# A two-layer hybrid decoder in float32: narrow matmuls for halved K, sums by a ones matmul, work moved to ScalarE, modulation paced by stage

## The chip, the cores and the metric

The kernel runs on one core of one Trainium2 chip. The metric is the device time of one launch in microseconds (us), the median of several runs. PE is TensorE, DVE is VectorE, ACT is ScalarE, POOL is GpSimd, SP is SyncE, whose queue issues the weight transfers.

## What is computed

Two decoder layers on 256 tokens of width 2048, in float32. Layer 0 mixes tokens by gated linear attention (GLA), layer 1 by softmax attention with a forget bias (FoX). After each mixer comes a gated MLP with a causal convolution of width 3. Every sub-layer's input is normalised, scaled and shifted, and its output gated, by vectors that are a product of the condition `c` with `w_mod` (2 x 2048 x 12288, some 200 MB).

```python
def reference(x, c, ...):
    cond = jax.nn.silu(c)
    for i in range(DEPTH):
        mod = (cond @ w_mod[i] + b_mod[i])[:, None, :]
        sh_m, sc_m, g_m, sh_f, sc_f, g_f = jnp.split(mod, 6, axis=-1)
        h = rmsnorm(x, norm_mix[i]) * (1.0 + sc_m) + sh_m
        ...                                   # y = gla_mixer(h, ...) or fox_mixer(h, ...)
        x = x + (1.0 + g_m) * y
        h = rmsnorm(x, norm_ffn[i]) * (1.0 + sc_f) + sh_f
        x = x + (1.0 + g_f) * conv_ffn(h, ffn_w_up[i], ffn_conv_w[i], ffn_conv_b[i], ffn_w_down[i])
    return rmsnorm(x, norm_final)
```

## The kernel before

Activations lie transposed: 16 tiles of 128 features by 256 tokens. Each float32 operand of the large products is split in two, a high part (the value rounded to fp32r) and a low part (the rest), and a product is high x high + high x low + low x high.

*Weights.* `next_w` takes the next weight tile (0.5 MB) of a list written out ahead (`plan`): SP loads it into one of five ring buffers, ACT casts it to the high part (line 110), DVE subtracts for the low part (line 111), up to three tiles ahead of use. `stream_p` (line 544) multiplies: a tile holds two K rows of 512 columns, so 8 blocks of 128 x 128. In a block the high part of the weights meets high and low operand side by side, 512 columns (line 554), and the low part the high operand, 256 columns (line 555). The two halves of the result stand next to each other in a double bank of PSUM, two such banks for a group of 512 columns, of three that there are; `gather` adds them up. `stream_b` (line 587) does the same for products whose result has tokens in rows. `narrow` (line 605) is a 16-column product by three 256-column matmuls (lines 614 to 616).

*Stages.* For GLA and the first six column groups of layer 0's up-projection, K is cut in two halves of 8 tiles (`BLOCKS`, `FIRST`), all columns for the first half and then all for the second, whose partial results are added in SBUF by DVE (line 582). So the first half can start before scale and shift of the second are known. In order: the start (0 to 62 us), GLA's products, first half to about 209 and second half to 390, GLA out (to 500), layer 0's up-projection (514 to 1025, the halved groups until 796), its down-projection (to 1283), FoX's products and attention (to 1718), FoX out (to 1814), layer 1's up-projection (to 2325) and down-projection.

*Modulation.* `mod_tasks` makes tasks of one `w_mod` tile (0.5 MB, in the same ring), each a product of the tile with a column of the condition, added up on DVE in `acc` (line 250 the first, line 252 the others). After 16 tiles a column sum over the partitions is wanted: `finish` transposes `acc` (line 265) and sums each block with an accumulating activation on ACT (line 274), or at the start with a reduction on DVE. The tasks wait in a queue; `tick`, called after each weight tile, takes as many as `pace["bg"]` says (0.64 means 64 for 100 weight tiles), and small pieces of other work (convolutions, attention heads) at the pace `pace["side"]`. `set_pace(n)` spreads what is queued over n weight tiles. `between` empties the queue between the two halves of the up-projection.

*Operands.* `make_h` makes the normalised, scaled and shifted operand h, 16 pieces per stage, on demand: DVE product (line 464), ACT for the high part (line 465), DVE again for the unrounded value (line 466), DVE for the low part (line 467). `token_rstd` is the reciprocal root before it (lines 426 to 434). `raw_operand` (lines 482, 483) splits the others.

*Order.* Each engine works off its own queue in order. The order in each queue is set when the program is built, by a planner that simulates the program with its own costs, within the data's dependences and the limits that the kernel adds by hand (`issue_after`).

## Time and profile before

| | us |
|---|---|
| median of 3 runs | 2592.15 (2590.53 to 2594.13) |
| the profiled execution | 2593.84 |
| its span, first to last instruction | 2592.1 |

The profile is one execution, recorded by the hardware. A row of a table by stage gives the stretch, its length, then for each engine its busy time and the number of instructions, then the granted TensorE clock as a share of 2.4 GHz, the mean busy share of the 16 DMA engines, and GB/s. A row of a timeline gives start, duration, engine, line, operation, the tiles that it writes and reads, and in brackets how long the engine stood idle before and what ended the wait. A matmul's duration includes its way through the array: the distance between two starts says what one costs in a row of them. A row of instruction groups gives busy time, mean ns of one, and idle time before them.

### The profile page before, as it was taken

To read this page: it belongs to the slowest core of one execution; us is meant where nothing else is said; L and a number is where in the kernel's file an instruction comes from. 1 tells how busy PE (TensorE), PEld (TensorE's weight loads), DVE (VectorE), ACT (ScalarE), POOL (GpSimd) and SP (SyncE) were. 2 spreads that over 40 slices of the span, in tenths; PEclk is the share of its full clock that TensorE was granted. 3 is DMA by queue.
4 is the path that set the end of the run, shared out by engine and by line. 5 is a ranking of instruction groups with operands and counts; after the bars stand their busy time and mean duration, and the time that the engine had idled before them with its cause. 6 is when DMAs were issued, how large, how long until landed. Compare 5 with 4: busy or idle time off the path is not lost.

```text
span 2592.1 us, 36814 instructions
## 1 busy us (share of the span) xinstructions
PE 2486.6 (96%) x13738; PEld 2139.2 (83%) x13738; DVE 2010.2 (78%) x2784; ACT 1288.2 (50%) x1964; POOL 18.1 (1%) x35
## 2 busy tenths in 40 slices
PE   6999998899999999899999999999899999999998
PEld 6887887788888888788888888778788888888887
DVE  7877988888789999877587888877877777767554
ACT  2447353445555565443454555543655555565332
POOL 0000000000000000000000000100000000000000
PEclk7999998899999999999999999999999999999999
DMA  8896877789567888898589988768577777765653
GB/s 335 276 311 218 294 235 255 247 293 324 178 186 259 295 295 295 269 305 299 178 267 307 305 269 229 215 228 267 171 221 229 226 224 225 223 196 195 191 189 116
DMA packets 267727, 637.67 MB, mean 246 GB/s; under 512 B 23449, under 2 KB 24459, under 8 KB 267164
## 3 DMA queue, kind: packets, MB, share of 16 engines
q1 hardware_dynamic: 267160, 635.17, 75.3%
q8 instruction: 108, 1.77, 0.3%
q14 instruction: 71, 0.58, 0.1%
q10 hardware_dynamic: 388, 0.15, 0.0%
HBM read 633.14 MB, written 2.10 MB: 245 GB/s over the span
## 4 chain that ended last, share of the span: by engine, by line
PE 72%; DVE 12%; DMA 10%; issue 3%; ACT 3%; DVEq 0%; SPq 0%; ACTq 0%
PE pa L554 38%; PE pa L555 19%; DMA wm<-in_w_mod_dram 7%; DVE wl L111 4%; PE pa L601 4%; PE pa L599 4%; PE pa L600 4%; DVE acc L252 3%; ACT wh L110 1%; DVE xT L624 1%; DMA w<-in_ffn_w_down_dram 1%; DMA w<-in_gla_w_in_dram 1%; DMA w<-in_ffn_w_up_dram 0%; PE pm L411 0%; PE pm L265 0%
## 5 line engine op out<-in xcount | busy, mean ns | idle before, releaser
L110 ACT CAST wh<-w 128x1024 fp32r<-128x1024 f32 x819 | 856.2, 1049 | 986.5 <-PE pa L554 429.5
L111 DVE TENSOR_TENSOR wl<-w,wh 128x1024 fp32r<-128x1024 f32 x819 | 994.4, 1218 | 368.0 <-ACT wh L110 361.4
L554 PE MATMUL pa<-h,wh 128*128 128x512 f32 x3584 | 1264.4, 399 | 15.9 <-DVE h L467 7.8
L555 PE MATMUL pa<-h,wl 128*128 128x256 f32 x3584 | 992.8, 282 | 6.7 <-DVE wl L111 6.6
L554 PEld LDWEIGHTS pa<-h,wh 128*128 128x128 f32 x3584 | 671.4, 189 | 169.3 <-ACT h L465 8.1
L555 PEld LDWEIGHTS pa<-h,wl 128*128 128x128 f32 x3584 | 681.9, 190 | 21.9 <-DVE wl L111 9.4
L554 PE MATMUL pa<-op,wh 128*128 128x512 f32 x1920 | 676.0, 398 | 18.9 <-DVE op L483 14.8
L555 PE MATMUL pa<-op,wl 128*128 128x256 f32 x1920 | 531.9, 281 | 4.2 <-DVE wl L111 4.2
L252 DVE SCALAR_TENSOR_TENSOR acc<-wm,cT,acc 128x1024 f32<-128x1024 f32 x352 | 450.7, 1280 | 104.9 <-DMA wm<-in_w_mod_dram 103.9
L554 PEld LDWEIGHTS pa<-op,wh 128*128 128x128 f32 x1920 | 359.8, 189 | 103.6 <-DVE op L483 15.2
L555 PEld LDWEIGHTS pa<-op,wl 128*128 128x128 f32 x1920 | 363.9, 190 | 9.5 <-DVE wl L111 6.0
L600 PE MATMUL pa<-wh,h 128*128 128x512 f32 x512 | 201.6, 394 | 0.0
L599 PE MATMUL pa<-wh,h 128*128 128x512 f32 x512 | 200.7, 393 | 0.0
L601 PE MATMUL pa<-wl,h 128*128 128x512 f32 x512 | 197.5, 394 | 0.1
L1081 ACT ACTIVATE y<-u,cw 128x256 f32<-128x256 f32 x176 | 99.0, 597 | 37.3 <-DVE u L585 22.0
L601 PEld LDWEIGHTS pa<-wl,h 128*128 128x128 f32 x512 | 96.5, 189 | 20.1 <-DVE wl L111 0.4
L599 PEld LDWEIGHTS pa<-wh,h 128*128 128x128 f32 x512 | 96.6, 189 | 19.3
L600 PEld LDWEIGHTS pa<-wh,h 128*128 128x128 f32 x512 | 96.5, 189 | 19.2
L1082 DVE SCALAR_TENSOR_TENSOR y<-u,cw,y 128x255 f32<-128x255 f32 x176 | 84.0, 477 | 0.0
L1084 DVE SCALAR_TENSOR_TENSOR y<-u,cw,y 128x254 f32<-128x254 f32 x176 | 82.6, 476 | 0.7
L585 DVE TENSOR_TENSOR u<-u,pa 128x512 f32<-128x512 f32 x112 | 75.7, 679 | 4.0 <-ACT u L584 3.9
L624 DVE SCALAR_TENSOR_TENSOR xT<-pa,mod,xT 128x256 f32<-128x256 f32 x128 | 53.1, 476 | 20.1 <-PE pa L555 20.1
(238 smaller groups left out, 1249.4 us busy)
## 6 DMA issues: line engine op xcount, KB each, us to landing
wm<-in_w_mod_dram SPq DMA_DIRECT2D x352, 512.0 KB, 5.1
w<-in_ffn_w_up_dram SPq DMA_DIRECT2D x352, 512.0 KB, 4.7
w<-in_ffn_w_down_dram SPq DMA_DIRECT2D x176, 512.0 KB, 5.1
w<-in_fox_w_in_dram SPq DMA_DIRECT2D x128, 512.0 KB, 5.3
w<-in_gla_w_in_dram SPq DMA_DIRECT2D x96, 512.0 KB, 4.9
wm<-in_w_mod_dram SPq DMA_DIRECT2D x16, 1024.0 KB, 12.3
w<-in_gla_w_out_dram SPq DMA_DIRECT2D x32, 512.0 KB, 5.5
w<-in_fox_w_out_dram SPq DMA_DIRECT2D x32, 512.0 KB, 5.6
```

Source lines behind the costliest of these rows:

```text
L110: nc.scalar.copy(out=hi, in_=src)
L111: order["v"] = nc.vector.tensor_tensor(out=lo, in0=src, in1=hi.bitcast(F32), op=ALU.subtract).ins
L252: nc.vector.scalar_tensor_tensor(out=st["a"], in0=wt[:, j, :], scalar=col, in1=st["a"], op0=ALU.mult, op1=ALU.add)
L554: nc.tensor.matmul(o, ws[0][:, ms], hl, start=first, stop=False, skip_group_check=True)
L555: nc.tensor.matmul(o[:, 0, :], ws[1][:, ms], hl[:, 0, :], start=False, stop=last, skip_group_check=True)
L599: nc.tensor.matmul(o, lh[:, ts_], wh[:, hs_], start=first, stop=False)
L600: nc.tensor.matmul(o, ll[:, ts_], wh[:, hs_], start=False, stop=False)
L601: nc.tensor.matmul(o, lh[:, ts_], wl[:, hs_], start=False, stop=last)
L624: nc.vector.scalar_tensor_tensor(out=xT[:, m, :], in0=ps[:, j, s_, :], scalar=modcol(l, key, m), in1=xT[:, m, :], op0=ALU.mult, op1=ALU.add)
L1081: nc.scalar.activation(y, u, AF.Identity, scale=cw[:, l * 3 + 2, r:r + 1], bias=cw[:, 6 + l, r:r + 1])
L1082: nc.vector.scalar_tensor_tensor(out=y[:, 1:], in0=u[:, :T - 1], scalar=cw[:, l * 3 + 1, r:r + 1], in1=y[:, 1:], op0=ALU.mult, op1=ALU.add)
L1084: nc.vector.scalar_tensor_tensor(out=y[:, 2:], in0=u[:, :T - 2], scalar=cw[:, l * 3, r:r + 1], in1=y[:, 2:], op0=ALU.mult, op1=ALU.add)
```

## The change

Seven edits. (1) `finish` multiplies each block of `acc` by a column of ones, one output column per block, and DVE adds the bias; where four K tiles were multiplied on PE already (`direct`), the sums go on top of them. (2) The first product of each `acc` is made on ACT. (3) In `token_rstd` the two token columns are computed together, three steps an iteration. (4) In `make_h`, for all pieces but the first two, ACT makes the scaled value and then its rounded copy; DVE keeps the first product and the low part. (5) `stream_p` gets a second form, `wide=False`, for the halved stages: three 256-column matmuls into one result, one double bank per group, which is copied or added as one instruction of 1024 columns. (6) In FoX, scalings of the normalised heads, the bias addition and the division by the row sum are made on ACT. (7) In layer 0's FFN the modulation pace is 0.3 per weight tile in the last part of the up-projection (0.64 before), and the rest is spread over the first 80 weight tiles of the down-projection; the side pace there is 1.0 (0.7 before).

```diff
-N1, N2, N3, N4 = 26, 151, 152, 156
+UPRATE = 0.3
+N1, N2, N3, N4 = 26, 80, 152, 156
...
                     elif k == direct:
                         st["a"] = accp.tile([P, 1024], F32, tag="acc", name=nm("acc"))[:, :width]
-                        nc.vector.tensor_scalar(out=st["a"], in0=wt[:, j, :], scalar1=col, scalar2=None, op0=ALU.mult)
+                        nc.scalar.activation(st["a"], wt[:, j, :], AF.Copy, scale=col)
...
-                red = tmp.tile([P, 8], F32, tag="red", name=nm("red"))
-                for q0 in range(0, mn, 4):
-                    pt = bank2("pt")[:, 0, :] if wide or defer else misc()
-                    for m in range(min(4, mn - q0)):
-                        nc.tensor.transpose(pt[:, m * P:(m + 1) * P], st["a"][:, (q0 + m) * P:(q0 + m + 1) * P],
-                                            ident)
-                    if wide:
-                        mq = min(4, mn - q0)
-                        nc.vector.tensor_reduce(out=red[:, q0:q0 + mq], in_=pt[:, :mq * P]
-                                                .rearrange("p (m k) -> p m k", k=P), axis=AX.X, op=ALU.add)
-                        continue
-                    for m in range(min(4, mn - q0)):
-                        blk = pt[:, m * P:(m + 1) * P]
-                        nc.scalar.activation(blk, blk, AF.Copy, accum_out=red[:, q0 + m:q0 + m + 1])
+                pt = st["p"] if direct else bank2("pt")[:, 0, :] if wide or defer else misc()
+                for m in range(mn):
+                    nc.tensor.matmul(pt[:, m:m + 1], st["a"][:, m * P:(m + 1) * P], one,
+                                     start=(m == 0 and not direct), stop=True, skip_group_check=True)
                 dst = mod[:, l * 6 + s, m0:m0 + mn]
                 b0 = l * 96 + s * KT + m0
-                nc.vector.tensor_tensor(out=dst, in0=red[:, :mn], in1=bm[:, b0:b0 + mn], op=ALU.add)
-                if direct:
-                    nc.vector.tensor_tensor(out=dst, in0=dst, in1=st["p"][:, :mn], op=ALU.add)
+                nc.vector.tensor_tensor(out=dst, in0=pt[:, :mn], in1=bm[:, b0:b0 + mn], op=ALU.add)
...
         for _ in range(3):
-            for i in range(2):
-                c1 = slice(i, i + 1)
-                nc.vector.tensor_scalar(out=t[:, c1], in0=q[:, c1], scalar1=q[:, c1], scalar2=v[:, c1],
-                                        op0=ALU.mult, op1=ALU.mult)
-            for i in range(2):
-                c1 = slice(i, i + 1)
-                nc.vector.tensor_scalar(out=q[:, c1], in0=t[:, c1], scalar1=1.5, scalar2=q[:, c1],
-                                        op0=ALU.subtract, op1=ALU.mult)
+            nc.vector.tensor_tensor(out=t, in0=q, in1=q, op=ALU.mult)
+            nc.vector.tensor_tensor(out=t, in0=t, in1=v, op=ALU.mult)
+            nc.vector.scalar_tensor_tensor(out=q, in0=t, scalar=1.5, in1=q, op0=ALU.subtract, op1=ALU.mult)
...
-            nc.scalar.activation(hi, t, AF.Identity, scale=sc, bias=sh)
-            nc.vector.tensor_scalar(out=t, in0=t, scalar1=sc, scalar2=sh, op0=ALU.mult, op1=ALU.add)
+            if m < 2:
+                nc.scalar.activation(hi, t, AF.Identity, scale=sc, bias=sh)
+                nc.vector.tensor_scalar(out=t, in0=t, scalar1=sc, scalar2=sh, op0=ALU.mult, op1=ALU.add)
+            else:
+                nc.scalar.activation(t, t, AF.Identity, scale=sc, bias=sh)
+                nc.scalar.copy(out=hi, in_=t)
             ins = nc.vector.tensor_tensor(out=lo, in0=t, in1=hi.bitcast(F32), op=ALU.subtract).ins
...
-    def stream_p(kts, c0, rhs, done=None):
-        ps = [bank2().rearrange("p j (s t) -> p j s t", s=2) for _ in range(2)]
+    def stream_p(kts, c0, rhs, done=None, wide=True):
+        ps = [bank2().rearrange("p j (s t) -> p j s t", s=2) for _ in range(2 if wide else 1)]
...
-            o = ps[m // 2][:, m % 2, :, :]
-            nc.tensor.matmul(o, ws[0][:, ms], hl, start=first, stop=False, skip_group_check=True)
-            nc.tensor.matmul(o[:, 0, :], ws[1][:, ms], hl[:, 0, :], start=False, stop=last, skip_group_check=True)
+            if wide:
+                o = ps[m // 2][:, m % 2, :, :]
+                nc.tensor.matmul(o, ws[0][:, ms], hl, start=first, stop=False, skip_group_check=True)
+                nc.tensor.matmul(o[:, 0, :], ws[1][:, ms], hl[:, 0, :], start=False, stop=last, skip_group_check=True)
+                return
+            o = ps[0][:, m // 2, m % 2, :]
+            nc.tensor.matmul(o, ws[0][:, ms], hl[:, 0, :], start=(first and m % 2 == 0), stop=False,
+                             skip_group_check=True)
+            nc.tensor.matmul(o, ws[0][:, ms], hl[:, 1, :], start=False, stop=False, skip_group_check=True)
+            nc.tensor.matmul(o, ws[1][:, ms], hl[:, 0, :], start=False, stop=last, skip_group_check=True)
...
-        return ps
-    def gather(dst, ps, add=False):
-        if add:
-            nc.vector.tensor_tensor(out=dst, in0=dst, in1=ps[:, :, 1, :], op=ALU.add)
-        else:
-            nc.scalar.copy(out=dst, in_=ps[:, :, 1, :])
+        return ps if wide else ps[0]
+    def gather(dst, ps):
+        nc.scalar.copy(out=dst, in_=ps[:, :, 1, :])
         nc.vector.tensor_tensor(out=dst, in0=dst, in1=ps[:, :, 0, :], op=ALU.add)
...
-            for b in range(4):
-                dst = parts[key][:, b, :]
-                if new:
-                    nc.scalar.copy(out=dst, in_=ps[b // 2][:, b % 2, :])
-                else:
-                    nc.vector.tensor_tensor(out=dst, in0=dst, in1=ps[b // 2][:, b % 2, :], op=ALU.add)
+            for tt in range(TT):
+                take(parts[key][:, 2 * tt:2 * tt + 2, :], ps[tt], new)
...
             for g in range(2):
-                ps = stream_p(kts, c0 + g * 512, h)
-                for b in range(2):
-                    gather(parts[key][:, g * 2 + b, :].rearrange("p (j t) -> p j t", j=2), ps[b], not new)
+                ps = stream_p(kts, c0 + g * 512, h, wide=False).rearrange("p j s t -> p j (s t)")
+                take(parts[key][:, 2 * g:2 * g + 2, :], ps, new)
+        def take(dst, ps, new):
+            if new:
+                nc.scalar.copy(out=dst, in_=ps)
+            else:
+                nc.vector.tensor_tensor(out=dst, in0=dst, in1=ps, op=ALU.add)
...
                             blk = (tt * 2 + hh // 4) * 4 + hh % 4
-                            nc.vector.tensor_scalar(out=tok4[:, blk, :], in0=tok4[:, blk, :],
-                                                    scalar1=rs[:, blk:blk + 1], scalar2=None, op0=ALU.mult)
+                            nc.scalar.activation(tok4[:, blk, :], tok4[:, blk, :], AF.Copy, scale=rs[:, blk:blk + 1])
...
-                nc.vector.tensor_scalar(out=s[:, 0:P], in0=p_[:, 0:P], scalar1=cumt[:, 0, hd:hd + 1],
-                                        scalar2=None, op0=ALU.add)
-                nc.vector.tensor_scalar(out=s[:, P:3 * P], in0=p_[:, P:3 * P], scalar1=cumt[:, 1, hd:hd + 1],
-                                        scalar2=None, op0=ALU.add)
+                nc.scalar.activation(s[:, 0:P], p_[:, 0:P], AF.Identity, bias=cumt[:, 0, hd:hd + 1])
+                nc.scalar.activation(s[:, P:3 * P], p_[:, P:3 * P], AF.Identity, bias=cumt[:, 1, hd:hd + 1])
...
-                nc.vector.tensor_scalar(out=s[:, 0:P], in0=s[:, 0:P], scalar1=mx[:, 6:7], scalar2=None, op0=ALU.mult)
-                nc.vector.tensor_scalar(out=s[:, P:3 * P], in0=s[:, P:3 * P], scalar1=mx[:, 7:8], scalar2=None,
-                                        op0=ALU.mult)
+                nc.scalar.activation(s[:, 0:P], s[:, 0:P], AF.Copy, scale=mx[:, 6:7])
+                nc.scalar.activation(s[:, P:3 * P], s[:, P:3 * P], AF.Copy, scale=mx[:, 7:8])
...
         def up(g, half, kts, add=False):
+            c0 = half * DFF + g * 512
             if half == 0 and not add:
                 us[g] = bigt([P, 8, T], "u")
-            ps = stream_p(kts, half * DFF + g * 512, h)
+            dst = us[g][:, half * 4:half * 4 + 4, :]
+            if kts is not ALL:
+                ps = stream_p(kts, c0, h, wide=False).rearrange("p j s t -> p (j s) t")
+                if add:
+                    nc.vector.tensor_tensor(out=dst, in0=dst, in1=ps, op=ALU.add)
+                else:
+                    nc.scalar.copy(out=dst, in_=ps)
+                return
+            ps = stream_p(kts, c0, h)
             for b in range(2):
-                m = half * 4 + 2 * b
-                gather(us[g][:, m:m + 2, :], ps[b], add)
+                gather(dst[:, 2 * b:2 * b + 2, :], ps[b])
...
+        down()
         add_residual(l, "g_f", list(range(FT)), rhs)
...
@@ -1240,7 +1240,14 @@
         queue(mod_tasks(0, "g_f"))
         queue_halves(1, "m")
         pace["bg"] = SLOW
-    ffn(0, lazy(make_h(0, "f"), KT, 2, (8,)), (ALL[:8], between, lambda: set_pace(N2)))
+    def after():
+        pace["bg"] = UPRATE
+    def down():
+        pace["side"] = 1.0
+        set_pace(N2)
+    ffn(0, lazy(make_h(0, "f"), KT, 2, (8,)), (ALL[:8], between, after), down)
```

## Rows read from the trace of the kernel before

**Rows 1.** The page, part 1: busy us, share of the span, instructions.

```profile
PE 2486.6 (96%) x13738; PEld 2139.2 (83%) x13738; DVE 2010.2 (78%) x2784; ACT 1288.2 (50%) x1964; POOL 18.1 (1%) x35
```

**Rows 2.** Table by stage, five stretches (columns as told above).

```profile
540.00:560.00 20.00, 20.00 (x116) 17.38 (x115) 17.91 (x17) 8.79 (x11) 0.00 (x0) 1.00 0.96 338
660.00:665.00 5.00, 4.89 (x15) 4.24 (x16) 5.00 (x16) 2.19 (x4) 0.00 (x0) 0.50 0.22 79
796.00:1025.00 229.00, 228.14 (x1308) 198.70 (x1307) 217.03 (x296) 134.41 (x212) 0.00 (x0) 1.00 0.87 294
1025.00:1283.00 258.00, 249.01 (x1422) 216.72 (x1422) 190.89 (x203) 111.45 (x152) 0.00 (x0) 0.99 0.83 277
1589.00:1718.00 129.00, 122.00 (x677) 101.95 (x676) 98.36 (x190) 67.32 (x133) 8.27 (x8) 0.97 0.74 203
```

**Rows 3.** Timeline of PE, seven entries before which it stood idle.

```profile
212.92 0.58 PE L614 MATMUL pm<-h,wh 128*128 128x256 f32 x1 [4.07 <-ACT h L465]
...
269.55 0.58 PE L555 MATMUL pa<-h,wl 128*128 128x256 f32 x1 [2.98 <-DVE wl L111]
...
413.10 0.79 PE L554 MATMUL pa<-op,wh 128*128 128x512 f32 x1 [5.67 <-DVE op L483]
...
503.03 1.05 PE L411 MATMUL pm<-ones,ss 128*128 128x1 f32 x8 [1.93 <-ACT pm L274]
...
660.11 0.76 PE L554 MATMUL pa<-h,wh 128*128 128x512 f32 x1 [4.27 <-DVE h L467]
...
1044.53 0.79 PE L554 MATMUL pa<-op,wh 128*128 128x512 f32 x1 [7.26 <-DVE op L483]
...
1824.38 0.76 PE L554 MATMUL pa<-h,wh 128*128 128x512 f32 x1 [0.94 <-ACT pt L274]
```

**Rows 4.** Groups of instructions by line and form, costs of single operations.

```profile
L110 ACT CAST wh<-w 128x1024 fp32r<-128x1024 f32 x816 | 854.9, 1051 | 981.6 <-PE pa L554 427.8 <-DMA w<-in_ffn_w_up_dram 92.7 <-DMA w<-in_ffn_w_down_dram 84.4
L252 DVE SCALAR_TENSOR_TENSOR acc<-wm,cT,acc 128x1024 f32<-128x1024 f32 x352 | 450.7, 1280 | 104.9 <-DMA wm<-in_w_mod_dram 103.9
...
L274 ACT ACTIVATE pm<-pm 128x128 f32<-128x128 f32 x144 | 37.5, 261 | 3.9 <-PE pm L265 3.1
...
L465 ACT ACTIVATE h<-hn,mod 128x256 fp32r<-128x256 f32 x64 | 35.7, 595 | 32.0 <-DVE hn L464 28.4 <-DVE mod L279 2.1 <-DVE mod L277 1.2
...
L274 ACT ACTIVATION_READ_ACCUMULATOR pm<-pm 128x1 f32 x144 | 26.9, 187 | 0.0
...
L466 DVE TENSOR_SCALAR hn<-hn,mod 128x256 f32<-128x256 f32 x64 | 25.1, 404 | 2.3 <-ACT h L465 2.3
...
L250 DVE TENSOR_SCALAR acc<-wm,cT 128x1024 f32<-128x1024 f32 x24 | 18.0, 749 | 13.5 <-DMA wm<-in_w_mod_dram 13.5
...
L582 DVE TENSOR_TENSOR u<-u,pa 128x512 f32<-128x512 f32 x24 | 16.2, 680 | 0.8 <-PE pa L555 0.8
...
L866 DVE TENSOR_TENSOR oT<-oT,pm 128x1024 f32<-128x1024 f32 x4 | 4.8, 1206 | 0.0
...
L460 ACT COPY rb<-pm 128x256 f32<-128x256 f32 x4 | 1.4, 355 | 21.9 <-DVE hn L464 21.9
```

**Rows 5.** Timeline of PE, two stretches: 256-column matmuls in threes, then pairs.

```profile
90.71 0.28 PE L614 MATMUL pm<-h,wh 128*128 128x256 f32 x1
...
93.52 0.40 PE L554 MATMUL pa<-h,wh 128*128 128x512 f32 x1
...
2000.25 0.40 PE L554 MATMUL pa<-h,wh 128*128 128x512 f32 x1
...
2003.71 0.40 PE L554 MATMUL pa<-h,wh 128*128 128x512 f32 x1
```

**Rows 6.** Timeline of DVE from 1818: a two-column step, then two iterations' first steps.

```profile
1818.15 0.17 DVE L424 TENSOR_SCALAR tq<-tq 128x2 int32<-128x2 int32 x1
1818.36 0.46 DVE L429 TENSOR_SCALAR tt<-tq,tv 128x1 f32<-128x1 f32 x2
...
1818.98 0.45 DVE L429 TENSOR_SCALAR tt<-tq,tv 128x1 f32<-128x1 f32 x2
```

4 lines of the change are left out of this document (2 added, 2 removed).

## The prediction

> **What bounds the kernel now.** I read the page's busy shares first [rows 1]: TensorE (PE) is busy 96% of the span, VectorE (DVE) 78%, ScalarE (ACT) 50%. A busy PE can only be shortened by giving it less to stream or by taking its stops away, so I went on to the table by stage [rows 2] and then to the PE timeline, keeping the entries before which PE stood idle [rows 3]. In rows 2 the last part of layer 0's up-projection (796 to 1025) has PE busy 228.14 of 229 us although DVE is at 217: DVE is nearly as full, yet PE hardly waits. The down-projection (1025 to 1283) lasts 258 us with PE busy 249. So averages say little; what can be won stands in rows 3, where PE stops, mostly at the seams between stages: 4.07 us before 212.92, 2.98 before 269.55, 5.67 before 413.10, 1.93 before 503.03, 4.27 before 660.11, 7.26 before 1044.53, 0.94 before 1824.38, together 27.1 us. A stop costs more than itself: the stretch 660 to 665, right after one, has a granted clock of 0.50 [rows 2], the 1.2 GHz level, so its 5 us do 2.5 us of work. I found 0.50 or 0.51 for 3 to 6 us after four of these stops (one row stands); I price it at 1.5 to 2.5 us a stop.
>
> **The change, part by part.**
>
> *Column sums by a ones matmul.* A finished sum of 1024 columns went through 8 transposes, 8 ACT activations with a read of the accumulator each (0.261 and 0.187 us, 64 us in all [rows 4]), and a DVE add. It now takes 8 one-column matmuls and the add. PE pays about the same: 8 one-column matmuls take 1.05 us at 503.03 [rows 3], and the 8 transposes that they replace load weights just as often. What goes is some 3 us of ACT per sum, in ACT's queue. The wait before 503.03 names these activations and goes: -2. Before 1824.38 they are named too: -0.9, and -1.5 of slow clock. Before 212.92 and 660.11 the wait is for the operand h, which needs the new scale and shift, and these needed the activations, which lay mixed with weight casts on ACT. About 1 us of h's own chain (0.595 + 0.355 on ACT [rows 4], then DVE) stays late, so each of the two loses 3 us and 2 us of slow clock: -10. Sum -14.4. Ends: -8 (h is late for its own chain) and -20 (all four stops and their clock gone).
>
> *Narrow form where K is halved.* Side by side, a block took a 512- and a 256-column matmul; 10 such pairs start between 2000.25 and 2003.71, 0.346 us a pair [rows 5]. Narrow, it takes three 256-column matmuls. The rank-16 projection has that very form: 24 of them lie between 90.71 and 93.52, 0.117 us each, 0.351 for three. 160 weight tiles (64 in GLA, 96 in the up-projection) of 8 blocks use it: 1280 x 0.005 = +6.4 us. Both forms stream 768 columns, so the low end is 0; I take +3. The form also halves the banks that a group holds and cuts its collection: a first group gave DVE 2 x 0.680 us [rows 4], now nothing (ACT copies 1024 columns at once); an adding group gave it 4 x 0.680, now one 1024-wide add of about 1.206. With 20 groups of each, DVE loses 27.2 + 30.3 = 57 us. Most falls where PE does not wait. It counts before 269.55, where PE waited 2.98 for DVE and four q and k adds lie ahead (4 x 1.5 = 6 us), and before 413.10 (four r adds, again 6 us, for a wait of 5.67). I take -3 and -4.5 with the clock, of at most -4.5 and -8; the other end is 0.
>
> The Trainium skill ("TensorE: Matmul & The Clock Gate", Back-to-back issue gap, and LDWEIGHTS behind it) says that a stream of weight loads and matmuls is paced by both, and that 128 columns load in about 107 ns. The one-column matmuls at 503.03 agree: 1.05 / 8 = 0.13 us, nearly all load. Read strictly, as loads that nothing hides, the third load per block would add 1280 x 0.107 = 137 us by the page. Rows 5 disagree: 0.117 us for 256 columns with a load of their own.
>
> *h on ScalarE.* For 56 of the 64 pieces of h, DVE loses a 0.404 us product and ACT gains a copy between 0.355 (a plain copy of 256 columns) and 0.595 us [rows 4]. Where a stage starts, a weight tile brings two pieces: ACT then needs 2 x (0.595 + 0.355) + 1.051 for the cast = 2.95 us against PE's 8 x 0.346 = 2.77, and DVE 0.8 less than before. I take -2 over all starts, from -6 to +5 (ACT late by 0.18 in 8 tiles of four starts).
>
> *First sums, attention scalings, the root.* 24 first products move from DVE (0.749) to ACT (about 1.05, as the cast of the same width); both lie beside transfers: 0, from -1 to +2. 128 small scalings of attention move to ACT, which is busy 67 of 129 us from 1589 to 1718, where DVE is busy 98 and PE lacks 7 [rows 2]; in a queue that is worked off in order they can also come late: -1.1, from -5 to +5. In the root a two-column step follows the last after 0.21 us and an iteration takes 0.62 [rows 6]; three joint steps take the same: 0.
>
> The skill speaks against these moves ("ScalarE: Activation LUTs", Rules for kernel authors: additions and products belong on VectorE). Rows 4 agree on the price of one: 0.595 against 0.404, 1.051 against 0.749. By the rule h on ScalarE would stand at its bad end, +5 for my -2, and the time at 2577.
>
> *Pace.* By the paces in the code the last 80 weight tiles of layer 0's up-projection took 51 of 96 modulation tiles (80 x 96/151) and now take 24; the 88 of the down-projection took 45 and now take 72, at 0.9 for each of the first 80. In the up-projection DVE gets 27 x 1.28 = 35 us lighter [rows 4], but PE can gain at most 229 - 80 x 2.77 = 7 us: -2.5. In the down-projection 1.9 transfers of 0.524 MB per 2.77 us would need 360 GB/s; the best stretch of this mix that I found moved 338 at a DMA share of 0.96 [rows 2]. At 338 a tile takes 0.996 / 338 = 2.95 us: 80 x 2.95 + 8 x 2.77 = 258 us, what the stage takes now with its stop of 7.26 us and the clock loss. That stop waits for an operand split queued on DVE; the side pace of 1.0 brings the last convolutions out in 4 weight tiles and not 6. With the stop gone the stage stays at 258, with it whole it grows by 9: +2.5. The good end is -9 (PE sets the pace); starved transfers stand below.
>
> Sum: -14.4 + 3 - 7.5 - 2 - 1.1 - 2.5 + 2.5 = -22.0 us. The profiled execution took 2593.84 us around a span of 2592.1, 1.7 over the median of 2592.15; its span would become 2570.1, and the median 2570.
>
> **The rivals.**
> *The down-projection starves.* All transfers pass through five ring buffers; one is free again only when its cast and split, or its product, is done. If supply stays at the 294 GB/s of the stage before [rows 2], a tile takes 0.996 / 294 = 3.39 us and the stage 293 us, 35 more than now; with the other gains (-24.5) the time is 2603. It decides below some 305 GB/s (79.7 MB in 261 us). For it: transfers already run there at a share of 0.83, and PE stops. Against: 338 GB/s with the same five buffers. 0.09.
> *The freed time falls idle.* The seams are bound by the chain of norm, root, broadcast and h; ACT and DVE get free but nothing starts earlier, as h stays behind the same casts. Only 503.03 and 1824.38 are won (-3) and the narrow form costs 3: 2592. For it: the waits before 212.92 and 660.11 name h, not the sums. 0.07.
> *The third load stands bare.* At 0.13 us each [rows 3], 1280 add 166 us: about 2733. Rows 5 speak against it. The rule on loads cited above would give this side. 0.02.
>
> **How the numbers follow.** My forecast has 0.82. A measurement of this kernel can tell about 0.2% (5 us) from no change. Faster 0.82; within 0.2% 0.07 (freed time idle); slower 0.09 + 0.02 = 0.11. The ends of the unknown costs add up to -60 and +19; all at one end is unlikely, so the range goes from 2543 (seams, clock and attention near their good ends) to 2597, which takes in the second rival and part of the first.
>
> **What would show it.** ACT's accumulating activations gone and PE's stops near 213, 503 and 660 us below 1.5 us: the sums. Narrow matmuls 0.117 us apart and their tiles at 2.77 to 2.85 us: the form. The down-projection at 255 to 262 us with transfers near 330 GB/s, the up-projection's last part at 226: the pace. I am wrong if these stops stay with h named, if the down-projection passes 270 us, or if tiles in the halved stages exceed 2.95 us.

## The result, and the profile after

| | before | after |
|---|---|---|
| median, us | 2591.47 (2590.53 to 2594.13, 5 runs) | 2603.57 (2599.43 to 2609.78, 5 runs) |
| the profiled execution (its span) | 2593.84 (2592.1) | 2600.83 (2598.8) |

After over before is 1.0046, 95% interval 1.0029 to 1.0063: some 12 us slower, where 2570 was forecast and 2597 was the upper end. A ratio of 0.0010 is 2.6 us; the us behind a ratio below are worked out so. The groups of experiments ran on different chips, each beside runs of the kernel before on its own chip, and the ratios are taken there. Stage tables are of one execution each: they show where the time lies, and differences of a few us in them say little.

The page of after, part 1, which answers [rows 1]. PE is 41 us busier and DVE 107 us less busy; the span has grown by 7:

```profile
PE 2527.9 (97%) x15210; PEld 2233.1 (86%) x15210; DVE 1903.7 (73%) x2451; ACT 1317.0 (51%) x1796; POOL 16.3 (1%) x35
```

The table by stage of after, for the last three stretches of [rows 2]: the up-projection's last part, the down-projection, and the stage with the attention.

```profile
783.00:1009.00 226.00, 226.00 (x1301) 198.04 (x1301) 185.40 (x259) 131.59 (x180) 0.00 (x0) 1.00 0.73 236
1009.00:1285.00 276.00, 262.72 (x1467) 224.46 (x1465) 218.31 (x229) 110.68 (x121) 0.00 (x0) 0.98 0.88 303
1604.00:1723.00 119.00, 118.12 (x683) 100.98 (x682) 83.45 (x122) 81.30 (x166) 4.34 (x8) 1.00 0.70 221
```

From the first matmul of each stage: after is 9.9 us ahead when the up-projection begins (504.1 for 514.0) and 15.6 ahead at the down-projection. The down-projection then takes 289.4 us to the first matmul of FoX, where it took 269.0: after is now 4.9 behind. FoX's products lose 10.6 more, the attention's stage wins 10.7 back, and the end is 6.7 late.

The PE timeline of after, entries with an idle time before them, where [rows 3] had its stops:

```profile
201.31 1.95 PE L264 MATMUL pm<-ones,acc 128*128 128x1 f32 x16 [0.86 <-DVE acc L253]
...
419.71 0.58 PE L545 MATMUL pa<-op,wl 128*128 128x256 f32 x1 [2.48 <-DVE wl L112]
...
469.99 0.38 PE L545 MATMUL pa<-op,wl 128*128 128x256 f32 x1 [2.10 <-DVE wl L112]
...
496.40 1.87 PE L400 MATMUL pm<-ones,sq 128*128 128x1 f32 x8 [1.63 <-ACT sq L387]
...
501.10 0.76 PE L358 MATMUL pm<-dg,ones 128*128 128x128 f32 x2 [2.83 <-DVE dg L356]
504.09 0.58 PE L548 MATMUL pa<-h,wh 128*128 128x256 f32 x1 [1.15 <-ACT h L450]
...
1018.12 0.80 PE L544 MATMUL pa<-op,wh 128*128 128x512 f32 x1 [3.06 <-DVE op L471]
...
1829.35 0.77 PE L544 MATMUL pa<-h,wh 128*128 128x512 f32 x1 [2.15 <-DVE h L455]
```

The stops of 4.07, 2.98, 5.67 and 4.27 us at 213, 270, 413 and 660 are gone, and 7.26 became 3.06. Before the squares' sums (503.03 before, 496.40 now) PE no longer waits for column sums, but 1.63 us for the squares themselves, and the last seam's 0.94 became 2.15. The stops before 419.71 and 469.99 are new. So four of the seven seams did what was said of them, and the time went elsewhere.

### The profile page after: what moved, and what is told of

It reads as the page before. It is cut to its first block, busy times and chain, and to the rows that moved or that the text cites. A ratio compares the mean times of both kernels' runs of the same rounds, so it can differ in the third digit from the quotient of the medians.

```text
span 2598.8 us, 39178 instructions
## 1 busy us (share of the span) xinstructions
PE 2527.9 (97%) x15210; PEld 2233.1 (86%) x15210; DVE 1903.7 (73%) x2451; ACT 1317.0 (51%) x1796; POOL 16.3 (1%) x35
## 4 chain that ended last, share of the span: by engine, by line
PE 74%; DMA 13%; DVE 9%; issue 3%; ACT 2%; SPq 0%; DVEq 0%; ACTq 0%
PE pa L544 28%; PE pa L545 14%; PE pa L551 5%; PE pa L550 5%; DMA w<-in_ffn_w_down_dram 5%; PE pa L548 5%; DMA wm<-in_w_mod_dram 5%; PE pa L594 4%; PE pa L593 4%; PE pa L592 4%; DVE wl L112 3%; DVE acc L253 3%; ACT wh L111 2%; DVE xT L617 1%; DMA w<-in_gla_w_out_dram 1%
## 5 line engine op out<-in xcount | busy, mean ns | idle before, releaser
L544 PE MATMUL pa<-h,wh 128*128 128x512 f32 x2304 | 810.6, 396 | 4.6 <-DVE h L455 4.2
L544 PEld LDWEIGHTS pa<-h,wh 128*128 128x128 f32 x2304 | 430.4, 188 | 102.5 <-DVE h L455 3.0
L548 PE MATMUL pa<-h,wh 128*128 128x256 f32 x1280 | 360.6, 282 | 2.0 <-ACT h L450 2.0
L550 PE MATMUL pa<-h,wh 128*128 128x256 f32 x1280 | 360.6, 282 | 0.6 <-DVE h L455 0.6
L548 PEld LDWEIGHTS pa<-h,wh 128*128 128x128 f32 x1280 | 242.8, 190 | 3.3 <-ACT h L450 2.4
L550 PEld LDWEIGHTS pa<-h,wh 128*128 128x128 f32 x1280 | 243.2, 190 | 2.0 <-DVE h L455 1.2
L592 PE MATMUL pa<-wh,h 128*128 128x512 f32 x512 | 205.5, 402 | 0.0
L593 PE MATMUL pa<-wh,h 128*128 128x512 f32 x512 | 205.2, 401 | 0.0
L592 PEld LDWEIGHTS pa<-wh,h 128*128 128x128 f32 x512 | 97.2, 190 | 23.1 <-ACT v L682 0.6
```

What stands on the lines that cost most here:

```text
L544: nc.tensor.matmul(o, ws[0][:, ms], hl, start=first, stop=False, skip_group_check=True)
L548: nc.tensor.matmul(o, ws[0][:, ms], hl[:, 0, :], start=(first and m % 2 == 0), stop=False, skip_group_check=True)
L550: nc.tensor.matmul(o, ws[0][:, ms], hl[:, 1, :], start=False, stop=False, skip_group_check=True)
L592: nc.tensor.matmul(o, lh[:, ts_], wh[:, hs_], start=first, stop=False)
L593: nc.tensor.matmul(o, ll[:, ts_], wh[:, hs_], start=False, stop=False)
```

## The experiments

**The pace, and what limits the down-projection.** First the pace alone on the kernel before, then the changed kernel without it.

```diff
+UPRATE = 0.3
-N1, N2, N3, N4 = 26, 151, 152, 156
+N1, N2, N3, N4 = 26, 80, 152, 156
...                                        # after() and down() as in the change
```

> The kernel before with the new pacing alone (0.3 of a background task a tick in the up-projection's last part, the rest spread over the first 80 ticks of the down-projection, side steps at 1.0 there). Theory 'the pace starves the down-projection': the down-projection goes from 269 to 285 to 295 us and the up-projection's last part from 228 to about 226, so 2591.5 + 14 to + 24 = 2606 to 2616 us; the old column sums on VectorE add to it if anything. Rival 'the down-projection lost its time to the other edits': it stays at 265 to 272 us and the time is 2587 to 2594 us.

Measured: 1.0054 (1.0036 to 1.0073), + 14 us. The down-projection to the first matmul of FoX takes 289.3 us, the up-projection's last part 225.3 for 228.3. The pace does this alone.

```diff
 def after():
-        pace["bg"] = UPRATE
+        set_pace(N2)                       # N2 = 151
 def down():
-        pace["side"] = 1.0
-        set_pace(N2)
+        pass
```

> The changed kernel with the pacing of before: one rate from the up-projection's last part through the down-projection, and the side steps at 0.7 a tick. Theory 'the pace starves the down-projection': the first block's down-projection goes back from 289 to about 269 us, the up-projection's last part from 226 back to about 228, so 2603.6 - 20.4 + 2.6 = about 2586 us (2581 to 2591). Rival 'the down-projection lost its time to the other edits' (the first sums on ScalarE, the halves waiting for ScalarE): the down-projection stays at 280 to 289 us although its loads are spread again, and the time is 2596 to 2606 us.

Measured: 1.0012 (0.9996 to 1.0029). The down-projection is back at 271.2 us, as the theory says; the other edits don't hold it up. The stage by the table, from its first matmul to FoX's, in e4 and then in e2:

```profile
1022.90:1312.16 289.26, 268.07 (x1478) 225.47 (x1476) 226.91 (x259) 121.47 (x197) 0.00 (x0) 0.98 0.85 291
```

```profile
1030.61:1301.79 271.18, 262.45 (x1488) 229.53 (x1486) 194.79 (x225) 113.17 (x127) 0.00 (x0) 0.97 0.77 263
```

But the time, 2599.30, is 8 us above the theory's upper end: the rest of the change, forecast at - 22, is worth nothing even without the pace. That is the second question, below.

Why does the stage starve? Two kernels take the background tasks' work apart, each run once: the first leaves these additions out of the result, the second loads half of each tile and uses it twice, with two additions where there was one.

```diff
-                    else:
+                    elif not cut[0]:        # True during layer 0's down-projection
                         nc.vector.scalar_tensor_tensor(out=st["a"], in0=wt[:, j, :], ...)
```

> The changed kernel in which, during the first block's down-projection, the background tasks load their weights as ever but all additions on VectorE except each block's first product are left out (some 70 tasks of two products, about 1.1 us each). Part of the computation is missing. Theory 'the transfers are the limit' (323 GB/s at 93% of the engines, 3.12 us a tile for 1.0 MB): the down-projection stays at 283 to 292 us. Rival 'VectorE or the ring slots that it holds are the limit': with 60 to 70 us of VectorE work less the stage falls to 265 to 274 us.

```diff
+                if cut[0] and kt > direct:
+                    src, dst_ = src[:, :width // 2], dst_[:, :, :width // 2]
...
+                        for o in (0, hw):
+                            nc.vector.scalar_tensor_tensor(out=st["a"][:, o:o + hw], in0=wt[:, j, :hw], ...)
```

> The changed kernel in which, during the first block's down-projection, each background load fetches half of its columns and VectorE adds that half twice, so that it has as many elements to add as ever. Part of the computation is replaced. Theory 'the transfers are the limit': a tile needs 0.52 MB of its own and about 0.24 of background, 2.4 us at 323 GB/s, under the 2.80 us of its matmuls, and the stage falls to 265 to 274 us. Rival 'VectorE is the limit': it stays at 283 to 292 us.

Measured: the down-projection took 272.7 us without the additions (2593.68 in all) and 295.5 with half the bytes (2620.80). The theory that transfers are the limit fell twice. The 200 us in the middle of the stage, in the table by stage, of the changed kernel and then of the one without the additions:

```profile
1060.00:1260.00 200.00, 193.70 (x1093) 165.88 (x1091) 157.02 (x154) 74.80 (x74) 0.00 (x0) 0.99 0.93 323
```

```profile
1060.00:1260.00 200.00, 198.62 (x1142) 173.47 (x1142) 97.09 (x101) 80.07 (x79) 0.00 (x0) 1.00 0.96 345
```

With the same loads to make, the transfers moved 345 GB/s instead of 323. The issue queue says what held them: what SP's queue waited for in these 200 us (line, releaser: us, times, longest), changed kernel first.

```profile
SPq L232 <- DVE wl L112: 70.2, 46, 2.6
SPq L508 <- DVE acc L253: 28.8, 37, 1.1
SPq L508 <- DVE wl L112: 23.4, 15, 2.4
```

```profile
SPq L233 <- DMA wm<-in_w_mod_dram: 61.4, 41, 3.3
SPq L509 <- DVE wl L112: 42.3, 46, 2.4
```

A load waits until one of the five slots is free, and DVE frees it. The changed kernel issued, in the same stretch (KB each, median us to landing):

```profile
w<-in_ffn_w_down_dram SPq DMA_DIRECT2D x64, 512.0 KB, 5.9
wm<-in_w_mod_dram SPq DMA_DIRECT2D x59, 512.0 KB, 5.9
```

123 loads in 200 us through five slots: each is held 5 / 0.615 = 8.1 us, 5.9 of them until the load has landed. That time alone is no proof, since a slot is also held while its tile waits for its turn. In the same 200 us the kernel before made 112 loads, 8.9 us a slot, and PE was fed:

```profile
1060.00:1260.00 200.00, 198.88 (x1143) 173.35 (x1143) 150.12 (x148) 82.09 (x97) 0.00 (x0) 1.00 0.88 298
```

So either the slots are too few for the loads of the new pace, or DVE is too slow; a sixth slot tells.

```diff
-RING = 5
+RING = 6
-SB = 4
+SB = 3
-T2 = 5
+T2 = 4
```

> The changed kernel with six ring slots for the weights instead of five (room for it: three score buffers instead of four and four square buffers instead of five in the attention and the norms); pacing and everything else as in the changed kernel. In the first block's down-projection it started 123 loads in 200 us, 0.615 a microsecond, so that each of the five slots was held 5/0.615 = 8.1 us, of which the landing is 5.9. Theory 'the slots are the limit, and VectorE holds them' (e6: without its sums the stage went back to 273 us at 345 GB/s): with six slots held as long there is room for 0.74 loads a microsecond, 2.6 us a tile, under the 2.82 of the matmuls; the stage falls from 289 to 266 to 276 us and the time to about 2583 to 2592 beside 2595 of the kernel before. Rival 'VectorE itself is the limit' (79% busy, its queue in the order of the tiles): more slots don't help, 283 to 292 us, 2600 to 2608.

Measured: 0.9973 (0.9962 to 0.9984), 2585.73 us, the down-projection at 272.6. Its middle 200 us, by the table and the issues:

```profile
1040.00:1240.00 200.00, 198.26 (x1147) 173.21 (x1146) 167.65 (x165) 80.86 (x83) 0.00 (x0) 1.00 0.96 342
```

```profile
w<-in_ffn_w_down_dram SPq DMA_DIRECT2D x68, 512.0 KB, 6.1
wm<-in_w_mod_dram SPq DMA_DIRECT2D x62, 512.0 KB, 6.0
```

DVE does more than in the starved stage (167.65 us for 157.02), nothing is left out, and PE is fed: it was neither the transfers nor DVE's throughput, but five slots, each held 8.1 us, from the issue over the landing to the release that stands in DVE's queue. The trace of e7 fits: 122 loads in 200 us, hardly other than the 123, though each landed after 4.3 to 4.8 us. By itself it shows less, since DVE had more to do there.

**The addresses.** In after the V-form matmuls (`stream_b`, which the change leaves alone in what PE does) stand 233 ns apart in every stage, before 227. The change drops the two 32-byte buffers `red`, so every scratch tile behind them lies 64 bytes lower.

```diff
+                tmp.tile([P, 8], F32, tag="red", name=nm("red"))      # in the changed kernel, unused
```

> The changed kernel with one thing more: the 64 bytes per partition that the old column sums took in the scratch pool (two 32-byte buffers, unused now) are kept free, so that every scratch tile behind them, the halves wh and wl among them, has the address that it had before. No instruction is added. Theory 'address': the V-form matmul (512 columns, wh moving) took 227 ns before and 233.4 ns after in every stage, in code that the change does not touch, because wh and wl moved by 64 bytes; with the old addresses it is 227 ns again, 1536 matmuls x 6.4 ns = 9.8 us come back, and the narrow form's 118.2 ns may fall towards the 116.8 ns that a 256-column matmul took before (3840 x 1.4 = 5.4 us): 2603.6 - 10 to - 15 = 2588 to 2594 us. Rival 'neighbours': the matmuls are slower because ScalarE now does more beside them, or the chip differed; then the cadence stays at 233 ns and the time at 2600 to 2607 us.

```diff
+    redp = ctx.enter_context(tc.tile_pool(name="redp", bufs=2))      # in the kernel before
-                red = tmp.tile([P, 8], F32, tag="red", name=nm("red"))
+                red = redp.tile([P, 8], F32, tag="red", name=nm("red"))
```

> The kernel before with one thing changed: the two 32-byte buffers of the old column sums are taken from a pool at the end of the memory, so that wh, wl and the other scratch tiles stand 64 bytes lower, at the addresses of the changed kernel. The instructions are the same. Theory 'address': the V-form matmul goes from 227 to 233 ns, + 9.8 us, and the wide form stays at 350.6 ns a pair (233.8 and 116.8 become about 231.5 and 119.2): 2591.5 + 10 = 2598 to 2604 us. Rival 'neighbours': the cadence stays at 227 ns and the time at 2589 to 2594 us.

The PE timeline of e1 and then of e3, the first and the last of 23 V-form matmuls in a row:

```profile
1369.79 0.39 PE L594 MATMUL pa<-wh,h 128*128 128x512 f32 x1
...
1374.77 0.39 PE L595 MATMUL pa<-wl,h 128*128 128x512 f32 x1
```

```profile
1369.64 0.40 PE L600 MATMUL pa<-wh,h 128*128 128x512 f32 x1
...
1374.77 0.40 PE L601 MATMUL pa<-wh,h 128*128 128x512 f32 x1
```

4.98 / 22 = 226 ns with the old addresses in the changed code, 5.13 / 22 = 233 with the new ones in the old code, both at a granted clock of 1.00: the addresses decide. For e3 the time follows (1.0054, 1.0037 to 1.0071, + 14; 1536 such matmuls make 9.8 of them). For e1 it does not: 1.0054 (1.0035 to 1.0074), where 2588 to 2594 us was expected. The narrow form pays at the old addresses. Narrow matmuls of after and then of e1, again 22 steps:

```profile
659.75 0.28 PE L551 MATMUL pa<-h,wl 128*128 128x256 f32 x1
...
662.34 0.28 PE L548 MATMUL pa<-h,wh 128*128 128x256 f32 x1
```

```profile
659.73 0.28 PE L549 MATMUL pa<-h,wh 128*128 128x256 f32 x1
...
662.37 0.28 PE L551 MATMUL pa<-h,wh 128*128 128x256 f32 x1
```

117.7 ns and 120.0; over 3840 of them 9 us (7 by the 118.2 of the whole stage). What V-form wins the narrow form loses.

```diff
+        hi, lo = hi[:, 8 * jh:8 * jh + n_], lo[:, 8 * jl:8 * jl + n_]   # jh, jl: 0 to 3 in turn
```

> The changed kernel with the pacing of before, in which the halves wh and wl are not always at the start of their buffers: four weight tiles in turn have wh 0, 32, 64 and 96 bytes further on, and the same for wl sixteen tiles at a time (the buffers are 128 bytes longer; the attention has three buffers for its scores instead of four to make room). The place in a line of 128 bytes is 96 at offset 0 (the changed kernel) and 32 at offset 64 (the kernel before). Theory 'the place in 128 bytes decides': the V-form matmul shows 233 ns where wh is at 96 and 227 where it is at 32, stage by stage mixed as the tiles come, and the places 0 and 64 fall into one of the two classes or give a third, faster one. The narrow form shows 118 ns at 96 and 120 at 32. Rival 'something else in the layout' (the other scratch tiles, the buffer, the rest of the address): no difference between the four offsets, all at 227 or all at 233.

Measured in one execution: over the sixteen combinations of places the median distance of two starts is 231 to 233 ns for V-form, nowhere 227, and 114 to 120 for the narrow form, in no two classes. So the place of wh and wl in a line of 128 bytes is not it, and the rival, something else in the layout, is left; which of the shifted tiles it is stays open.

**The parts alone**, each on the kernel before at its old addresses, against the term of the sum.

```diff
+            o = ps[0][:, m // 2, m % 2, :]                            # e10: the narrow form
...
-                        nc.scalar.activation(blk, blk, AF.Copy, accum_out=red[:, q0 + m:q0 + m + 1])
+                    nc.tensor.matmul(pt[:, m:m + 1], st["a"][:, m * P:(m + 1) * P], one, ...)   # e11
...
+                nc.scalar.activation(s[:, 0:P], p_[:, 0:P], AF.Identity, bias=cumt[:, 0, hd:hd + 1])   # e12
...
+                nc.scalar.activation(t, t, AF.Identity, scale=sc, bias=sh)                       # e13
...
-                        nc.vector.tensor_scalar(out=st["a"], in0=wt[:, j, :], scalar1=col, ...)
+                        nc.scalar.activation(st["a"], wt[:, j, :], AF.Copy, scale=col)           # e14
```

> The kernel before with the narrow form alone (three 256-column matmuls a block where K is split, one bank, one addition), at the old addresses. The prediction's term for it: + 3 us on the PE and - 7.5 us at the two seams, - 4.5. With the 120.0 ns that a narrow matmul took at the old addresses in e1 (360 a block beside 350.6) 1280 blocks cost + 12 us, not + 3: 'the cadence eats it': + 12 - 7.5 = + 4.5, ratio 1.0010 to 1.0030. Rival 'as predicted': 0.9975 to 0.9990. Rival 'the additions that go from VectorE and ScalarE are worth more than the seams' (e1 less its pace was at 1.000, e8, which lacks only the narrow form and the pace, at 1.002): 0.9965 to 0.9985.

> The kernel before with the column sums by the ones matmul alone, the scratch tiles at their old addresses. The prediction's term: - 14.4 us (ratio 0.9945; ends - 8 and - 20). Rival 'the time falls idle' (e8 gained 4 to 5 us up to 360 us and had lost them at 517, in the out-projection of the first mixer, where the stops at 405 and 413 us remained): the stops after the sums go, others behind them grow, 0.9985 to 1.0010. Rival 'the clock' (after 137.2 us the changed kernel's 16 one-column matmuls and the wait ahead of them were followed by some 4 us at half the clock): a loss of 2 to 4 us at each place where a wait stands ahead of them, 1.0005 to 1.0025.

> The kernel before with the attention's scalings on ScalarE alone, at the old addresses. The prediction's term: - 1.1 us (ends - 5 and + 5). In the changed kernel the attention's own stage (the output gate's projection) was 10.7 us shorter, in e8 5.9, while the stage ahead of it was 1.4 to 3.9 us longer. Theory 'VectorE was late there': - 5 to - 7, ratio 0.9973 to 0.9981. Rival 'the gain there is the other edits'' (the operand on ScalarE, the narrow form's fewer additions): 0.9990 to 1.0010.

> The kernel before with the normalised operand on ScalarE alone (from the third column block on: the scaled sum written by ScalarE, the high part copied from it by ScalarE, VectorE left with the product and the difference), at the old addresses. The prediction's term: - 2 us (ends - 6 and + 5). The edits measured so far leave a remainder: all but the narrow form and the pace together were at + 5.2 us (e8), the column sums alone at - 4.1 and the attention alone at - 1.3, so that this edit, the first sums and the root together would cost + 10.6. Theory 'the operand costs it' (ScalarE's two passes stand in a row ahead of the low part, where before the two engines worked side by side): + 6 to + 11 us, 1.0023 to 1.0042. Rival 'it is in the meeting of the edits, not in this one': 0.9992 to 1.0010.

> The kernel before with the first product of each background block on ScalarE alone, at the old addresses. The prediction's term: 0. Theory 'the first sums cost the remainder' (ScalarE, on whose copies of wh the PE waits, is held for 1.2 us once in each block): + 5 to + 10 us, 1.0019 to 1.0039. Rival 'nothing': 0.9990 to 1.0010.

And all of them but the narrow form and the pace, together (run before the parts were):

> The kernel before with the column sums by the ones matmul, the first sums, the scalings and the normalised operand on ScalarE and the shorter root, but with the side-by-side form where it was, the old pacing, and every scratch tile at its old address. Theory 'the seams gained what was forecast and three prices ate it' (pace + 14 to + 15, V-form addresses + 9.8, narrow matmuls + 5.4): without the three the gain stands alone, some 12 to 16 us below the kernel before: ratio 0.9938 to 0.9955, about 2580 us beside 2595. Rival 'the narrow form gave the seams' gain, as forecast (- 7.5 there, - 4.5 net)': 2586 to 2593 us. Rival 'there is no such gain' : 2593 to 2600 us.

| | term of the sum | measured ratio (95%) | us |
|---|---|---|---|
| e10 narrow form | - 4.5 | 0.9960 (0.9947 to 0.9972) | - 10.4 |
| e11 column sums | - 14.4 | 0.9984 (0.9975 to 0.9994) | - 4.1 |
| e12 attention | - 1.1 | 0.9995 (0.9987 to 1.0004) | - 1.3 |
| e13 operand | - 2 | 0.9978 (0.9966 to 0.9989) | - 5.7 |
| e14 first sums | 0 | 1.0035 (1.0022 to 1.0048) | + 9.1 |
| e8 all but narrow and pace | - 17.5 | 1.0020 (1.0008 to 1.0031) | + 5.2 |

e10 came out beyond the best of its expectations, though its matmuls stood 120.0 ns apart; e11 lies at the edge of its rival 'the time falls idle', and e12 in the range of its rival, that the gain seen in the attention's stage comes from other edits. e13 refuted the theory that the operand costs the remainder, and gained more than its rival allowed. e8 came out with its rival, 'there is no such gain'. e14 has the size of its theory, but not by the way that it named, ScalarE being held by a first sum. Much of what e14 loses lies in the out-projection of the first mixer: 129.1 us for 123.3, and for 124.1 to 127.1 in five other traces with the old sums (e3, e4, e10, e12, e13). The DVE timeline, kernel before and then e14: the last step of the group norm's root and the diagonal that needs it.

```profile
397.52 0.14 DVE L361 TENSOR_TENSOR grs<-rt,grs 128x4 f32<-128x4 f32 x1
...
401.13 0.47 DVE L367 TENSOR_SCALAR dg<-ident,grs 128x128 f32<-128x128 f32 x2
```

```profile
409.00 0.15 DVE L361 TENSOR_TENSOR grs<-rt,grs 128x4 f32<-128x4 f32 x1
409.07 1.28 DVE L252 SCALAR_TENSOR_TENSOR acc<-wm,cT,acc 128x1024 f32<-128x1024 f32 x1
410.27 0.47 DVE L367 TENSOR_SCALAR dg<-ident,grs 128x128 f32<-128x128 f32 x2
```

The first sums nearest to it are those at 351.92 and 449.90. In e14 the root's small steps of 0.15 us are queued later, between subtractions for wl and additions of 1.28, and the diagonal comes 9 us later: PE waits 7.03 us for it in e14, by its timeline:

```profile
410.61 1.22 PE L369 MATMUL pm<-dg,ones 128*128 128x128 f32 x4 [7.03 <-DVE dg L367]
```

The order laid down at build time differs. That this order is the cause is argued from one trace and not shown by a run; it stands for 2 to 6 of the 9.1 us.

**Together, and with six slots.** First three parts that gain alone, with five slots and with six.

> The kernel before with the three edits that gained alone (the narrow form - 10.4 us, the column sums - 4.1, the attention - 1.3), at the old addresses, with the old pacing, the old operand and the old first sums. Theory 'they add': - 15.8 us, ratio 0.9930 to 0.9950, about 2577 to 2580 beside 2592.7. Rival 'each frees the same time' (the narrow form and the sums both shorten the first mixer's stages, where the last wait then is the supply): 0.9950 to 0.9965.

> The same three edits with six ring slots (and three score buffers and four square buffers to make room; all scratch tiles stand 2048 bytes higher than at their old addresses). In the changed kernel the sixth slot was worth 0.0073 of the time (e9 0.9973 beside 1.0046), of which about 17 us in the down-projection that the new pace had starved and some 7 us in the first mixer's out-projection. Theory 'the slot helps where the supply was last, in the first mixer too': 6 to 10 us under the five slots, 0.9895 to 0.9925. Rival 'it only repaired what the pace had broken': within 0.0010 of the five slots.

Measured: 1.0002 (0.9992 to 1.0012) with five, outside both its expectations, and 0.9957 (0.9942 to 0.9973) with six. Alone the parts gain 15.8 us, together with five slots nothing. Parts that free the same time would still leave the 10.4 of the narrow form. Here the sums and the attention, added to it, cost 0.0042 (e10 to e15), 10.9 us, not far from the 8.6 that the sums cost below. Which of the two spoils it with five slots was not tried. With the sixth slot 11.7 us come out (0.0045). In these two traces 8.4 of them lie ahead of the up-projection (which begins at 510.8 us in e15, at 502.4 in e16), but four executions of one code up to there (after, e2, e6, e7) begin it between 504.1 and 514.7. That the slots were last in the first mixer too is therefore likely, not shown.

What the new column sums cost stands in the groups of PE, by form: those of the kernel before, and then of after (busy us, mean ns, idle before).

```profile
L265 PE MATMUL pm<-ident,acc 128*128 128x128 f32 x144 | 19.2, 273 | 0.6 <-DVE acc L252 0.6
L265 PE MATMUL pt<-ident,acc 128*128 128x128 f32 x48 | 10.6, 393 | 10.0 <-DVE acc L252 9.4 <-ACT pt L274 0.6
```

```profile
L264 PE MATMUL pm<-ones,acc 128*128 128x1 f32 x288 | 33.4, 246 | 1.4 <-DVE acc L253 1.4
L264 PE MATMUL pt<-ones,acc 128*128 128x1 f32 x64 | 12.3, 327 | 0.0
L264 PE MATMUL pd<-ones,acc 128*128 128x1 f32 x32 | 7.3, 353 | 2.0 <-DVE acc L253 2.0
```

The 192 transposes were one pass each; 192 float32 matmuls show 384, and as many weight loads. Busy 53.0 us for 29.8: + 23. The last two kernels differ in the column sums alone.

```diff
 # both: narrow form, operand, attention's scalings, old first sums, old pace, six slots
 # e17: the column sums of before       e18: the ones matmul
```

> The kernel before with the narrow form, the operand and the attention's scalings, with the old column sums, the old first sums and the old pacing, and six ring slots (three score buffers and four square buffers). The traces count the column sums: 192 transposes in 29.4 us of PE before, 384 one-column passes in 51.0 us in the changed kernel (0.79 us a block of 1024 columns then, 1.70 now), + 21.6 us of PE. Theory 'the ones matmul costs the PE what it saves ScalarE': where the waits for the supply are shortened by the sixth slot, those 21.6 us stand on the path, and this kernel is 4 to 12 us under its twin with the new sums: 2566 to 2576 us, ratio 0.9900 to 0.9935. Rival 'the new sums keep their gain of e11' (- 4.1): this kernel is 2 to 6 us over its twin, 2580 to 2586.

> The twin of e17 with the new column sums: the narrow form, the operand, the attention's scalings and the ones matmul, the old first sums and the old pacing, six ring slots. Beside e16 it has the operand on ScalarE in addition, which gained 5.7 us alone (e13). Theory 'the operand's gain stays': 2574 to 2578 us, ratio 0.9925 to 0.9945. Rival 'it is the same time that the others free' (as in e15): 2579 to 2584 us. Beside e17: theory 'the ones matmul costs the PE' 4 to 12 us slower, rival 2 to 6 us faster.

Measured: e17 2569.47 us (2567.38 to 2572.35), 0.9908 (0.9894 to 0.9922); e18 2578.15, 0.9941 (0.9927 to 0.9956). The ones matmul costs 0.0033, 8.6 us, once the supply is no longer last; e18 is 4 us under e16, which lacks the operand, with intervals that overlap. Part 1 of the page, e17 and then e18:

```profile
PE 2487.3 (97%) x15018; PEld 2205.3 (86%) x15018; DVE 1912.6 (75%) x2496; ACT 1342.1 (52%) x2124; POOL 17.1 (1%) x35
```

```profile
PE 2517.7 (98%) x15210; PEld 2238.2 (87%) x15210; DVE 1914.0 (74%) x2490; ACT 1293.4 (50%) x1772; POOL 16.1 (1%) x35
```

PE is busy 30 us less in e17, ACT 49 more. e17 beats the changed kernel and the one before; that its time is the one forecast for the change is chance, since it lacks four of the seven edits and has a slot more.

## Why the prediction was wrong, point by point

*The pace (forecast 0, measured + 14): the step that failed most.* The up-projection's part was right (- 2.5 forecast, - 3.0 in e4). For the down-projection the working took 338 GB/s, the best stretch of 20 us [rows 2], as what the five buffers can supply, 2.95 us a tile. The stage drew 323 and took 3.12 a tile (64 in 200 us). It lasted 289 us where 269 stood, although its 7.26 us stop shrank to 3.06. The rival "the down-projection starves" had named the cause, a buffer that is free only when cast and split or product are done, but priced it by a rate of another stage and got a chance of 0.09. That its 2603 is the measured time is luck: it is made of + 35 for the stage, which lost 20, and of - 24.5 for the rest, which gained nothing. The limit shows in the time that a slot is held (landing, then the queue of DVE): at 8.1 us five slots make 0.62 loads a microsecond, and 1.9 loads a tile want 0.69. The 8.1 is from the trace of after; before, the slots were held 8.9 with PE fed. The said sign, the down-projection beyond 270 us, came (276 in the table above).

*The column sums (- 14.4; - 4.1 alone, + 8.6 in e17 and e18).* Two steps failed. "PE pays about the same" read the row at 503.03 [rows 3] as eight matmuls; it is four of two passes, and the sums cost PE 23 us more, with twice the weight loads and not "just as often". On the path the price shows in FoX's products, where three sums lie: 0.91 us more for each make 2.7. This stretch, to the first matmul of the attention's stage, in e12 (transposes) and e11 (the ones matmul alone):

```profile
1291.81:1585.61 293.80, 293.57 (x1353) 241.11 (x1353) 228.58 (x311) 173.80 (x323) 4.29 (x7) 0.99 0.87 281
```

```profile
1281.81:1579.09 297.28, 297.15 (x1380) 245.03 (x1381) 243.19 (x376) 144.74 (x198) 4.55 (x8) 0.99 0.87 278
```

Wherever V-form ran at 227 ns it took 293.8 to 295.2 us with transposes (seven traces) and 297.3 to 299.5 with the ones matmul (six). And the gain of 10 at 212.92 and 660.11: those stops went, as expected, but what they freed did not always come through. The up-projection's last part began 14.7 us early in e11 and 13.0 in after, but 3.1 and 5.5 early and 2.2 late in three other executions of after's code up to there (e7, e6, e2). From that start to the end e11 then took 8.0 us longer than the kernel before (1803.6 for 1795.6), and 14 of the 24 sums lie there: in the end PE's price ate the gain. So the size came near that of the rival "the freed time falls idle" (0.07), but in e11 not in its way.

There is a price on top that no term had. In after, PE waited 0.50 us for the 16 one-column passes of one sum; its timeline, and the table by stage around and behind them:

```profile
137.20 1.95 PE L264 MATMUL pm<-ones,acc 128*128 128x1 f32 x16 [0.50 <-DVE acc L253]
```

```profile
136.00:139.00 3.00, 2.50 (x19) 2.02 (x19) 3.00 (x3) 0.31 (x1) 0.00 (x0) 1.00 0.75 218
139.00:141.00 2.00, 2.00 (x8) 1.20 (x8) 0.41 (x1) 2.00 (x3) 0.00 (x0) 0.69 0.84 270
141.00:143.00 2.00, 2.00 (x5) 1.60 (x6) 1.23 (x1) 1.59 (x2) 0.00 (x0) 0.50 0.83 260
```

The granted clock falls to 0.50, the 1.2 GHz level, with PE busy. In e8, where the same 16 passes came without a wait, it stayed at 1.00, as it did behind the eight transposes of the kernel before:

```profile
139.00:141.00 2.00, 2.00 (x13) 1.73 (x13) 0.40 (x1) 1.61 (x4) 0.00 (x0) 1.00 1.00 342
141.00:143.00 2.00, 2.00 (x10) 1.67 (x9) 0.98 (x1) 1.00 (x1) 0.00 (x0) 1.00 0.92 295
```

That column group took 26.6 us in after and 22.7 before. Its mean clock was 0.94, which makes some 1.6 us of the difference (an estimate); the rest is the wait, the passes and the slower V-form matmuls.

*The narrow form (- 4.5; - 10.4 alone).* The direction was right, the terms weren't. The blocks cost 3 x 118.2 = 354.6 ns for 350.6 at the new addresses, + 5 us, and 360.0, + 12, at the old: above the + 3 taken, and at the old addresses above its end of + 6.4. In e10's trace the halved blocks end 1.4 us late (797.9 for 796.5), so some 10.6 of the + 12 were won back up to there (an estimate), although 4.53 us still stand at the seam of 413. The gain as a whole lies behind: the down-projection took 265.7 us for 269.0 and the attention's stage 120.9 for 129.5, though no narrow matmul is in either; why is open.

*The operand (- 2; - 5.7).* Right sign, inside its ends. The Trainium skill ("ScalarE: Activation LUTs", Rules for kernel authors) would keep products and additions on VectorE, and the prediction gave that + 5. For the operand the runs speak against the rule.

*First sums, attention, root.* The attention was right (- 1.1; - 1.3). The first sums were given 0, from - 1 to + 2, and cost 9.1: the working priced 24 instructions by their own time, and not what another order of DVE's queue does to a chain behind it. The sign is that of the rule just cited; the row shows the order, not the price of one. The root was not tried alone.

*What no step had.* A removed buffer moved 64 bytes of addresses: + 9.8 us for V-form, of which 96 of its 128 tiles, 7.4 us, explain most of the 10.6 that FoX's products lost, and the 2.7 of the three sums the rest. The narrow matmul's gap between the two layouts gives 7 to 9 back in after.

*The sum.* The parts were added as if each had its own stop. Alone they make + 14 - 10.4 - 4.1 - 1.3 - 5.7 + 9.1 = + 1.6; e15 shows three of them at + 0.5 together instead of - 15.8. At the old addresses the whole change costs what its pace alone costs (e1 and e4, both 1.0054). Of the 34 us between forecast and result (- 22 and + 12) the pace makes 9 (after beside e2) to 14 (e4). The rest is gains that the parts show, if at all, alone. In the range nothing stood for parts that spoil each other's gain.

## What to carry to other kernels

When loads share a ring, price the ring, not only the bandwidth: slots divided by the time one must be held, from issue over landing to the release in a busy engine's queue, against the loads that a tile wants. Take that time where the consumer starves: in a fed stage a slot also waits for its turn, and the time held (8.9 us here) is no limit. Don't add up the gains of seams of one stretch before asking what is last once the first is gone, and what another part's price takes. Count the passes that a float32 matmul shows before calling a replacement equal.

## What the runs showed of the hardware

Moving scratch tiles by 64 bytes, with the instructions the same, changed the distance of 512-column matmuls from 227 to 233 ns and of 256-column ones from 120.0 to 118.2, at a granted clock of 1.00. 2048 bytes above the old place (e17) they show 227 and 120.0 again, 2048 above the new one (e9) 233 and 118. What in the layout does it is open.

A float32 matmul of one column shows as two entries, 1.70 us for eight blocks, where eight transposes of 128 columns take 0.79.

The transfers moved 345 GB/s over 200 us at a busy share of 0.96 (e6), with PE at 199 of 200 us beside them: what looked like full transfers at 0.93 and 323 GB/s had 7% in it that the slots did not use.
